# A hybrid decoder step: the decode tokens in the second token group, their state update beside groups three and four

## Chip, cores, metric

The kernel runs on one core of one Trainium2 chip. The metric is the device time of one execution in microseconds (us), as a median over repeated runs.

## What is computed

One inference step of a two-layer decoder on 1040 prompt tokens (16 meta tokens and 1024 own) and 8 decode tokens, one for each of 8 sequences with a state of their own. Layer 0 mixes tokens by a causal convolution, layer 1 by RWKV-7; each is followed by a squared-ReLU MLP (1024 to 4096 to 1024). All data are float32. The part that matters here is the RWKV-7 step, for 16 heads of size 64:

```python
def _wkv7_step(S, inp):
    r_t, w_t, k_t, v_t, kk_t, a_t = inp
    sa = jnp.einsum('bhvk,bhk->bhv', S, -kk_t)
    S = (S * w_t[:, :, None, :] + sa[..., None] * (kk_t * a_t)[:, :, None, :]
         + v_t[..., None] * k_t[:, :, None, :])
    y = jnp.einsum('bhvk,bhk->bhv', S, r_t)
    return S, y
...
r = (xr @ w_r).astype(f32)     # k, v likewise; decay, a and the gate g by low-rank products
...
y = jnp.moveaxis(ys, 0, 1)     # then a norm over each head, a bonus term, the gate and w_o
out = ((yn + bonus).astype(h.dtype) * g) @ w_o
```

For the prompt the state starts at zero and the kernel works in chunks of 64 tokens, with matrix products. For each decode token there is one such step from a given state, `state_wkv` (8 x 16 heads, 64 x 64 each), whose new value is an output.

## The kernel before

**Stages.** Layer 0 (convolution and MLP) takes the first part of the span. Then come the mixers of layer 1 (`mixer_in`, about 1130 to 1840 us), which make r, k, v, decay, rate and gate, and then per token group the output norm, `mixer_out` (w_o) and the second MLP. The features lie on the 128 partitions in 8 blocks (`KT`), the tokens along the free axis.

**Groups.** The mixers take the tokens in four groups (`G1`, L33; the code counts from 0): 272, 256, 256 and 264. The last one holds 256 prompt tokens and the 8 decode tokens. For each group and each feature block p, TensorE multiplies with w_r and w_v, and between these with w_k for the next group (`keys`). Before block 0 come the low-rank products for the gate (`gate`) and, in block 0, those for decay and rate (`decay_rate`); their weights are eight tiles of 256 KB per group (`narrow_w`, L930), loaded from a scratch in DRAM (d_lr) into the pool `wide` with four buffers (L771), gate first. k, the gate and the bonus go to DRAM (d_k, d_g, d_bv); k is fetched again (`fetch`). The operands of the recurrence go to DRAM too (d_ab, d_n, d_v).

**The recurrence.** `chunk(c)` (L1218) is a chain of small products on TensorE with steps on ScalarE and VectorE between them; `front(c)` loads its operands and masks them (ps "A", copies "no" L1198, masks "xa" L1199 and "nr" L1200; "sw" L1266 is the decayed state, a product on GpSimd). `inverses` (L1141) inverts small triangular blocks on VectorE for the four chunks of a group. Chunks, inverses and the output norm (`norm_gate`, L1397) are Python generators. Their pieces are issued between the large products: each fill point in the mixers calls `tick` (L1465), which advances the inverses by one step, the chunks by a credit of 2.0 and the first output norm by one step. A fill point stands before each block's projections and twice in each of them. What is left of the chunks runs beside `mixer_out` and the MLP of the first output group, through `filler`, together with the decode step and the output norms, each stream spread over all its points.

**Order.** On TensorE the instructions keep the order of the program (`manual_schedule`, L1471). On the other engines and DMA queues a planner orders them, by its own estimate of when each is ready; a queue then runs in that order, and an instruction that waits holds up those behind it. Semaphores come from the data dependencies. A tile whose pool has one buffer can be written again only when all readers of the last contents are done.

**Decode.** In the last group the columns behind the prompt (`npr` to `n`) are the decode tokens. Six vectors of each feature block (decay, k, key norm, its product with the rate, r, v) are copied to `ddec` by GpSimd (`dd`, L977). `decode_step` (L1354) then transposes `ddec` (four pieces, PSUM tag "x"), writes them to d_dec in DRAM and loads them again with (sequence, head) on the partitions (dq). Sixteen rounds follow, one for four of the 64 rows of each head's state: load the rows (128 x 256), two products with a sum along the row (`sa`, `yd`), five more products and additions, store. All nine operations are on VectorE (L1383 to L1391), load and store are issued by SyncE. The tiles live in a pool of their own (`dk`) that opens when the step begins.

The functions that the change touches:

Of the kernel before, what the change touches and what calls it, by code (L numbers as in the profile page):

```python
# [16 lines left out]
P = 128  # L17
# [15 lines left out]
G1 = [(0, 272), (272, 256), (528, 256), (784, 264)]  # L33
# [15 lines left out]
def hybrid_step(tc, x_prompt, x_sample, state_conv, state_shift, state_wkv, meta_tokens,  # L49
# [10 lines left out]
    with ctx:  # L60
# [710 lines left out]
        wide = pool(ld, "wided", 4)  # L771
# [6 lines left out]
        open_ep(ld, "d", ey=2)  # L778

# [14 lines left out]
        prep, norm = {}, {}  # L794
        sst = cur["raw"].tile([P, D], F32, name="sst", tag="raw")
# [10 lines left out]
        def shift_out(hx, npr):  # L806

            so = cur["raw"].tile([P, D], F32, name="so", tag="raw")
            for half in range(2):
                pv = bank(f"pso{half}")  # L810
                for q in range(4):
                    nc.tensor.transpose(pv[:DEC + 1, q * P:(q + 1) * P], hx[:, half * 4 + q, npr:npr + DEC + 1], ident)
                nc.scalar.copy(so[:DEC + 1, half * 512:(half + 1) * 512], pv[:DEC + 1, :])
            nc.scalar.dma_start(o_shift_prompt[0], so[0:1, :])
            nc.scalar.dma_start(o_shift_sample[0], so[1:DEC + 1, :])

        def prepare(g):

            c0, n = G1[g]
            npr = min(c0 + n, NP_TOK) - c0  # L820
            nm = lambda s, *a: f"{s}{g}" + "".join(f"_{x}" for x in a)

            hx = hnp.tile([P, KT, 1 + N1], F32, name=nm("hx"), tag="hx")
            if g == 0:
                nc.gpsimd.memset(hx[:, :, 0:1], 0.0)
                nc.sync.dma_start(hx[:, :, 1:1 + n], d_hn[:, :, :n])
            else:
                nc.sync.dma_start(hx[:, :, :1 + n], d_hn[:, :, c0 - 1:c0 + n])
            yield
            xx = hnp.tile([P, KT, N1], F32, name=nm("xx"), tag="xx")  # L830
            for k in range(KT):
                (nc.gpsimd if k % 3 == 2 else nc.vector).tensor_sub(xx[:, k, :npr], hx[:, k, 0:npr], hx[:, k, 1:1 + npr])
                yield
            if npr < n:
                nc.vector.tensor_sub(xx[:, :, npr:n], sps, hx[:, :, 1 + npr:1 + n])
            def mix(i, k):

                t = mixp.tile([P, N1], F32, name=nm("mx", i, k), tag="mx")
                nc.vector.scalar_tensor_tensor(t[:, :n], xx[:, k, :n], vec("x_mix", i * KT + k), hx[:, k, 1:1 + n],
                                               op0=ALU.mult, op1=ALU.add)  # L840
                return t[:, :n]

            prep[g] = mix, hx
# [26 lines left out]
        def keys(g, fill):  # L870

            c0, n = G1[g]
# [24 lines left out]
            split(*r16p, r16[:, :n], nc.vector)  # L897
        carry = {"tail": lambda: None}

        def mixer_in(g, tick):  # L900

            c0, n = G1[g]
            npr = min(c0 + n, NP_TOK) - c0
# [83 lines left out]
            def finish(p, rk, ab, vv):  # L987
                def trace():
# [10 lines left out]
                    pieces = [(i, a0 + i * P, P) for i in range(ncg // 2)] + ([(2, 0, META)] if g == 0 else [])  # L999
                    for i, c1, w in pieces:  # L1000
                        nc.tensor.transpose(pv_[:w, i * P:(i + 1) * P], vv[:, c1:c1 + w], ident)
# [33 lines left out]
                    bv = t_("bv", p, "bv", 2)  # L1035
                    nc.vector.tensor_mul(bv[:, :n], vv[:, :n], pb[:, :n])
                    return lambda: nc.gpsimd.dma_start(d_bv[:, p, c0:c0 + n], bv[:, :n])
# [8 lines left out]
            for p, rk2 in ahead_of(fetch):  # L1046
# [8 lines left out]
                gt = t_("gt", p, "gt", 2)  # L1055
                nc.scalar.copy(gt[:, :n], ps[:, :n])
                nc.scalar.dma_start(d_g[:, p, c0:c0 + n], gt[:, :n])
# [17 lines left out]
                em = t_("em", p, "em", 2)  # L1075
# [54 lines left out]
        st = {"done": -1, "inv": -1, "credit": 0.0, "decoded": False}  # L1130
# [223 lines left out]
        def decode_step():  # L1354

            with ExitStack() as s:
                dk = pool(s, "dk", 1)
                for q in range(4):
                    pt = bank(f"pdd{q}", "x")
                    for i in range(2):  # L1360
                        nc.tensor.transpose(pt[:6 * DEC, i * P:(i + 1) * P],
                                            ddec[:, 2 * q + i].rearrange("p i b -> p (i b)"), ident)
                    dst = tt(f"dst{q}", "t2")[:6 * DEC, :256]
                    nc.scalar.copy(dst, pt[:6 * DEC, :256])
                    nc.scalar.dma_start(d_dec.rearrange("i b d -> (i b) d")[:, q * 256:(q + 1) * 256], dst)
                    yield 3
                dq = dk.tile([P, 6, HS], F32, name="dq")
                nc.scalar.dma_start(dq, d_dec.rearrange("i b (h c) -> (b h) i c", c=HS))
                yield 6
                sa = dk.tile([P, HS], F32, name="sa")  # L1370
                yd = dk.tile([P, HS], F32, name="yd")
                HV = HS // 16
                s_in = state_wkv[0].rearrange("b h v k -> (b h) v k")
                s_out = o_wkv_sample[0].rearrange("b h v k -> (b h) v k")
                rows = lambda t: t.rearrange("p (v k) -> p v k", k=HS)
                for hv in range(HS // HV):
                    vs = slice(hv * HV, (hv + 1) * HV)
                    S = rows(dk.tile([P, HV * HS], F32, name=f"Sdec{hv}", tag="S", bufs=2))
                    t4 = rows(dk.tile([P, HV * HS], F32, name=f"t4{hv}", tag="t4"))
                    nc.sync.dma_start(S, s_in[:, vs, :])  # L1380
                    overv = lambda i: dq[:, i:i + 1, :].broadcast_to([P, HV, HS])
                    overk = lambda t: t.unsqueeze(2).broadcast_to([P, HV, HS])
                    nc.vector.tensor_mul(t4, S, overv(2))  # L1383
                    nc.vector.tensor_reduce(sa[:, vs], t4, axis=AX.X, op=ALU.add)
                    nc.vector.tensor_mul(S, S, overv(0))
                    nc.vector.tensor_mul(t4, overk(sa[:, vs]), overv(3))
                    nc.vector.tensor_add(S, S, t4)
                    nc.vector.tensor_mul(t4, overk(dq[:, 5, vs]), overv(1))
                    nc.vector.tensor_add(S, S, t4)
                    nc.vector.tensor_mul(t4, S, overv(4))  # L1390
                    nc.vector.tensor_reduce(yd[:, vs], t4, axis=AX.X, op=ALU.add)  # L1391
                    nc.sync.dma_start(s_out[:, vs, :], S)
                    yield 4
                nc.scalar.dma_start(d_y[NP_TOK:].rearrange("b (h c) -> (b h) c", c=HS), yd)
                st["decoded"] = True
# [66 lines left out]
        ng0 = norm_gates(GN_OF[0])  # L1462
        PACE = [0, 2.0, 2.0, 2.0]

        def tick(g, slow):  # L1465
# [3 lines left out]
            next(ng0, None)  # L1469

        in_order = lambda: tc.manual_schedule(engines={nc.tensor.engine})  # L1471
        with in_order():
# [7 lines left out]
            carry["tail"]()  # L1480
            while invert():
# [7 lines left out]
        with ExitStack() as l1:  # L1489
# [81 lines left out]
            def group(g, actp, hidp, sums):  # L1571
# [8 lines left out]
                                ([decode_step()], 82), ([norm_gates(GN_OF[1]), ng2], NGA))  # L1580
# [64 lines left out]
```

## Time and profile before

| | us |
|---|---|
| median of 3 runs | 2832.22 (2829.05 to 2835.45) |
| the profiled execution | 2823.53 |
| its span, first to last instruction | 2821.8 |
| mean granted TensorE clock in it | 0.977 of full speed |

The profile is of one execution. PE is TensorE, PEld its weight loads, DVE VectorE, ACT ScalarE, POOL GpSimd, SP SyncE; a q behind a name (SPq, ACTq) marks what the engine's queue issues, such as DMAs. The rows come from these views: the page with 40 equal slices (a digit is the busy share in tenths, PEclk the granted clock in tenths); busy time by stretch (start:end, length, then busy time and number of instructions for each engine, granted clock, share of time that the DMA engines were busy, GB/s); waits (engine, operation, line, what it waited for: us in total, times, the longest); groups (line, engine, operation, output<-inputs, shapes, count | busy us, mean ns of one | idle before, and for what); one line's instructions (count: shortest, median, longest in ns, first and last start); the order in time (start, length, instruction, [idle before <- releaser]); and the chain that ended last, where a DMA's row gives its start and how long it took.

### The profile page before, as it was taken

How to read it: one execution, taken by the hardware profiler on the slowest of the kernel's cores; microseconds unless marked ns; L12 is line 12 of the kernel's file. 1: busy time of each engine (PE TensorE's matmuls, PEld its weight loads, DVE VectorE, ACT ScalarE, POOL GpSimd, SP SyncE). 2: the span in 40 equal slices, each digit the busy share in tenths (PEclk: the TensorE clock that was granted, in tenths of full speed). 3: DMA queues.
4: the chain of work that ended last, by engine and by line, in shares of the span. 5: the costliest groups of instructions: out<-in, count | busy, mean ns of one | idle time of the engine just before them, and what ended most of it. 6: DMA issues, size and time to landing. Idle time of an engine off the chain costs nothing.

```text
span 2821.8 us, 51604 instructions
## 1 busy us (share of the span) xinstructions
PE 2669.5 (95%) x19594; PEld 2521.3 (89%) x19594; DVE 1785.4 (63%) x3586; ACT 1189.5 (42%) x2235; POOL 1520.2 (54%) x2100
## 2 busy tenths in 40 slices
PE   8999999999999899998999999978899999999998
PEld 8999999999999898786877778777899999999998
DVE  5999999996455545234756455588985564444444
ACT  5545444544354343233454454454444452222223
POOL 6686877887788775022212112375568773333332
PEclk9999999999999999999999999989899999999999
DMA  6663544454445642677767766766665542222211
GB/s 179 179 184 87 156 137 134 137 175 137 140 132 162 191 130 82 198 215 201 185 176 211 186 172 178 203 184 167 170 202 155 170 125 87 68 69 73 70 53 42
DMA packets 615862, 416.42 MB, mean 148 GB/s; under 512 B 104936, under 2 KB 558760, under 8 KB 615614
## 3 DMA queue, kind: packets, MB, share of 16 engines
q1 hardware_dynamic: 565996, 367.36, 46.0%
q10 hardware_dynamic: 41090, 19.93, 2.7%
q0 software_dynamic: 8528, 25.83, 2.6%
q8 instruction: 155, 2.54, 0.4%
q14 instruction: 93, 0.76, 0.1%
HBM read 345.60 MB, written 68.37 MB: 147 GB/s over the span
## 4 chain that ended last, share of the span: by engine, by line
PE 71%; DVE 13%; DMA 6%; issue 4%; ACT 3%; POOL 2%; SPq 0%; ACTq 0%; DVEq 0%; POOLq 0%
PE ps_in L187 8%; PE ps_in L189 8%; PE ps_in L188 8%; PE out L187 8%; PE out L189 8%; PE out L188 8%; PE pk L865 3%; PE pr L865 2%; PE pv L865 2%; POOL wo_lo L162 1%; DVE ni L1154 1%; DVE cv L519 1%; PE ps_o L189 1%; DVE tt L1153 1%; PE ps_o L188 1%
## 5 line engine op out<-in xcount | busy, mean ns | idle before, releaser
L162 POOL TENSOR_TENSOR wo_lo<-wo_raw,wo_hi 128x256 fp32r<-128x256 f32 x736 | 566.5, 802 | 267.5 <-ACT wo_hi L157 253.2
L162 POOL TENSOR_TENSOR wi_lo<-wi_raw,wi_hi 128x256 fp32r<-128x256 f32 x640 | 488.9, 796 | 285.8 <-ACT wi_hi L157 265.4
L187 PE MATMUL out<-hh,wo_hi 128*128 128x352 f32 (+2 forms) x1536 | 503.4, 328 | 19.8 <-DVE h L355 9.3
L355 DVE TENSOR_TENSOR h<-h,out 128x352 f32<-128x352 f32 (+2 forms) x768 | 387.7, 511 | 195.9 <-PE out L189 195.2
L189 PE MATMUL out<-hl,wo_hi 128*128 128x352 f32 (+2 forms) x1536 | 494.0, 324 | 7.2 <-DVE hl L141 7.2
L187 PE MATMUL ps_in<-m_h,wi_hi 128*128 128x352 f32 (+2 forms) x1536 | 496.2, 323 | 1.2 <-DVE h L355 1.2
L188 PE MATMUL out<-hh,wo_lo 128*128 128x352 f32 (+2 forms) x1536 | 495.3, 323 | 0.0
L189 PE MATMUL ps_in<-m_l,wi_hi 128*128 128x352 f32 (+2 forms) x1536 | 494.5, 322 | 0.1
L188 PE MATMUL ps_in<-m_h,wi_lo 128*128 128x352 f32 (+2 forms) x1536 | 492.6, 321 | 0.0
L519 DVE SCALAR_TENSOR_TENSOR cv<-u,wdw,cv 128x352 f32<-128x352 f32 (+2 forms) x720 | 377.2, 574 | 0.7
L157 ACT CAST wi_hi<-wi_raw 128x1024 fp32r<-128x1024 f32 x160 | 167.9, 1050 | 388.6 <-PE out L189 198.3
L157 ACT CAST wo_hi<-wo_raw 128x1024 fp32r<-128x1024 f32 x184 | 192.6, 1049 | 318.4 <-PE out L189 153.6
L187 PEld LDWEIGHTS out<-hh,wo_hi 128*128 128x128 f32 x1536 | 293.0, 191 | 26.0 <-DVE h L355 11.6
L189 PEld LDWEIGHTS out<-hl,wo_hi 128*128 128x128 f32 x1536 | 291.2, 190 | 8.9 <-DVE hl L141 8.8
L188 PEld LDWEIGHTS out<-hh,wo_lo 128*128 128x128 f32 x1536 | 292.4, 190 | 0.7
L187 PEld LDWEIGHTS ps_in<-m_h,wi_hi 128*128 128x128 f32 x1536 | 290.1, 189 | 3.2 <-issue 1.7
L188 PEld LDWEIGHTS ps_in<-m_h,wi_lo 128*128 128x128 f32 x1536 | 289.4, 188 | 1.0
L189 PEld LDWEIGHTS ps_in<-m_l,wi_hi 128*128 128x128 f32 x1536 | 288.7, 188 | 1.2 <-DVE m_l L285 0.4
L342 DVE SCALAR_TENSOR_TENSOR r<-ps_in,rs_m 128x352 f32<-128x352 f32 (+2 forms) x192 | 98.4, 516 | 238.7 <-PE ps_in L189 235.0
L141 DVE TENSOR_TENSOR hl<-s,hh 128x352 fp32r<-128x352 f32 (+2 forms) x192 | 147.1, 767 | 106.2 <-ACT hh L140 106.0
L344 ACT ACTIVATE s<-r 128x352 f32<-128x352 f32 (+2 forms) x192 | 93.8, 491 | 129.1 <-DVE r L342 128.5
L865 PE MATMUL pv<-mx,wv_raw 128*128 128x256 f32 (+2 forms) x512 | 125.3, 393 | 2.7 <-ACT rk L1049 2.7
(356 smaller groups left out, 4874.4 us busy)
## 6 DMA issues: line engine op xcount, KB each, us to landing
wi_raw<-in_w_mlp_in_dram SPq DMA_DIRECT2D x160, 512.0 KB
wo_raw<-in_w_mlp_out_dram SPq DMA_DIRECT2D x160, 512.0 KB
wk_raw<-in_rwkv_w_k_dram SPq DMA_DIRECT2D x32, 512.0 KB
wr_raw<-in_rwkv_w_r_dram SPq DMA_DIRECT2D x32, 512.0 KB
wv_raw<-in_rwkv_w_v_dram SPq DMA_DIRECT2D x32, 512.0 KB
d_ab<-ab POOLq DMA_DIRECT2D x32, 512.0 KB, 5.0
pg_raw<-in_conv_w_pw_dram SPq DMA_DIRECT2D x24, 512.0 KB
pa_raw<-in_conv_w_pw_dram SPq DMA_DIRECT2D x24, 512.0 KB
```

Of the source, the lines that this page charges most:

```text
L141: eng_lo.tensor_sub(lo, src, hi.bitcast(F32))
L157: nc.scalar.copy(hi[:, :a * b], raw[:, :a * b])
L162: eng_lo.tensor_sub(lo[:, cs], raw[:, cs], hi[:, cs].bitcast(F32))
L187: nc.tensor.matmul(ps, w[0], act[0], start=first, stop=False)
L188: nc.tensor.matmul(ps, w[1], act[0], start=False, stop=False)
L189: nc.tensor.matmul(ps, w[0], act[1], start=False, stop=last)
L342: nc.vector.scalar_tensor_tensor(r[:, :n], ps[:, :n], 0.0, rs()[:, :n], op0=ALU.max, op1=ALU.mult)
L344: nc.scalar.activation(s[:, :n], r[:, :n], AF.Square)
L355: nc.vector.tensor_add(hv[:, 4 * i + m, :], hv[:, 4 * i + m, :], ps[:, :n])
L519: nc.vector.scalar_tensor_tensor(acc[m][:, :n], ug[:, m, j:j + n], wdw[:, m, j:j + 1], acc[m][:, :n], op0=ALU.mult, op1=ALU.add)
L865: nc.tensor.matmul(ps[:, :n], w[:, k, :], act[k], start=k == 0, stop=k == KT - 1)
L1153: nc.vector.tensor_mul(o, ni[:, :j, j:j + 1].broadcast_to([B, j, wd]), ni[:, j:j + 1, j + 1:top].broadcast_to([B, j, wd]))
```

## The change

The 8 decode tokens leave the last group and join the second (`GD = 1`): the groups are now 272, 256 + 8, 256, 256. Their columns in DRAM are no longer next to the group's own, so each load or store of a whole group becomes two there (`pieces`): hx, d_k written and fetched, d_g, d_bv. `shift_out` runs twice, for the decode tokens in group 1 and for the last prompt token in group 3. `decode_step` becomes a generator that `tick` advances in groups 2 and 3, with a credit of 1.25 per fill point; what is left would run right behind the mixers. Its seven products and additions per round go to GpSimd, the two reductions stay on VectorE. The store of the state is issued by GpSimd. The transposes use the PSUM tag of the projections. The pool `dk` now lives as long as the mixers; `wide` has three buffers instead of four, and bv, gt and em have one instead of two.

```diff
-G1 = [(0, 272), (272, 256), (528, 256), (784, 264)]
+G1 = [(0, 272), (272, 256), (528, 256), (784, 256)]
+GD = 1
...
-        wide = pool(ld, "wided", 4)
+        wide = pool(ld, "wided", 3)
...
         open_ep(ld, "d", ey=2)
+        dk = pool(ld, "dk", 1)
...
+        def extent(g):
+            c0, npr = G1[g]
+            return c0, npr, npr + (DEC if g == GD else 0)
+
+        def pieces(g):
+
+            c0, npr, n = extent(g)
+            return [(slice(0, npr), slice(c0, c0 + npr))] + ([(slice(npr, n), slice(NP_TOK, T))] if n > npr else [])
...
-        def shift_out(hx, npr):
+        def shift_out(hx, lo, n, dst):
...
+            if npr < n:
+                nc.sync.dma_start(hx[:, :, 1 + npr:1 + n], d_hn[:, :, NP_TOK:])
...
-                nc.scalar.dma_start(d_k[:, p, c0:c0 + n], k_[:, :n])
+                for ts, cs in pieces(g):
+                    nc.scalar.dma_start(d_k[:, p, cs], k_[:, ts])
...
-                    bv = t_("bv", p, "bv", 2)
+                    bv = t_("bv", p)
                     nc.vector.tensor_mul(bv[:, :n], vv[:, :n], pb[:, :n])
-                    return lambda: nc.gpsimd.dma_start(d_bv[:, p, c0:c0 + n], bv[:, :n])
+                    return lambda: [nc.gpsimd.dma_start(d_bv[:, p, cs], bv[:, ts]) for ts, cs in pieces(g)]
...
-                nc.sync.dma_start(rk2[:, 1, :n], d_k[:, p, c0:c0 + n])
+                for ts, cs in pieces(g):
+                    nc.sync.dma_start(rk2[:, 1, ts], d_k[:, p, cs])
...
-                gt = t_("gt", p, "gt", 2)
+                gt = t_("gt", p)
                 nc.scalar.copy(gt[:, :n], ps[:, :n])
-                nc.scalar.dma_start(d_g[:, p, c0:c0 + n], gt[:, :n])
+                for ts, cs in pieces(g):
+                    nc.scalar.dma_start(d_g[:, p, cs], gt[:, ts])
...
-                em = t_("em", p, "em", 2)
+                em = t_("em", p)
...
+                if g == GD and p == 0:
+                    shift_out(hx, 1 + npr, DEC, o_shift_sample[0])
                 if g == 3 and p == 2:
-                    shift_out(hx, npr)
+                    shift_out(hx, npr, 1, o_shift_prompt[0])
...
+            eng = nc.gpsimd
+            for hv in range(HS // HV):
+                vs = slice(hv * HV, (hv + 1) * HV)
+                S = rows(dk.tile([P, HV * HS], F32, name=f"Sdec{hv}", tag="S", bufs=2))
+                t4 = rows(dk.tile([P, HV * HS], F32, name=f"t4{hv}", tag="t4"))
+                nc.sync.dma_start(S, s_in[:, vs, :])
+                yield 1
+                eng.tensor_mul(t4, S, overv(2))
+                nc.vector.tensor_reduce(sa[:, vs], t4, axis=AX.X, op=ALU.add)
+                eng.tensor_mul(S, S, overv(0))
+                yield 1
+                eng.tensor_mul(t4, overk(sa[:, vs]), overv(3))
+                eng.tensor_add(S, S, t4)
+                yield 1
+                eng.tensor_mul(t4, overk(dq[:, 5, vs]), overv(1))
+                eng.tensor_add(S, S, t4)
+                nc.gpsimd.dma_start(s_out[:, vs, :], S)
+                yield 1
+                eng.tensor_mul(t4, S, overv(4))
+                nc.vector.tensor_reduce(yd[:, vs], t4, axis=AX.X, op=ALU.add)
+                yield 1
+            nc.scalar.dma_start(d_y[NP_TOK:].rearrange("b (h c) -> (b h) c", c=HS), yd)
...
         def tick(g, slow):
...
+            if g > GD:
+                st["dec"] += 1.25 * slow
+                while st["dec"] > 0 and not st["decoded"]:
+                    st["dec"] -= next(dec, 0)
...
             carry["tail"]()
+            for _ in dec:
+                pass
...
-                                ([decode_step()], 82), ([norm_gates(GN_OF[1]), ng2], NGA))
+                                ([norm_gates(GN_OF[1]), ng2], NGA))
```

The four transposes and the load of dq ahead of the rounds stay as they were, with credits of 3 each and 6.

More of the change, by code (lines that the diff above doesn't have):

```diff
@@ L1354, in decode_step @@
         def decode_step():
[L1356 to L1395, printed above, removed]
@@ new lines, in decode_step @@
+            for q in range(4):
+                pt = bank(f"pdd{q}")
+                for i in range(2):
+                    nc.tensor.transpose(pt[:6 * DEC, i * P:(i + 1) * P],
+                                        ddec[:, 2 * q + i].rearrange("p i b -> p (i b)"), ident)
+                dst = pr.tile([P, N1], F32, name=f"dst{q}", tag="st", bufs=2)[:6 * DEC, :256]
+                nc.scalar.copy(dst, pt[:6 * DEC, :256])
+                nc.scalar.dma_start(d_dec.rearrange("i b d -> (i b) d")[:, q * 256:(q + 1) * 256], dst)
+                yield 3
@@ new lines, in decode_step @@
+            dq = dk.tile([P, 6, HS], F32, name="dq")
+            nc.scalar.dma_start(dq, d_dec.rearrange("i b (h c) -> (b h) i c", c=HS))
+            yield 6
+            sa = dk.tile([P, HS], F32, name="sa")
+            yd = dk.tile([P, HS], F32, name="yd")
+            HV = HS // 16
+            s_in = state_wkv[0].rearrange("b h v k -> (b h) v k")
+            s_out = o_wkv_sample[0].rearrange("b h v k -> (b h) v k")
+            rows = lambda t: t.rearrange("p (v k) -> p v k", k=HS)
+            overv = lambda i: dq[:, i:i + 1, :].broadcast_to([P, HV, HS])
@@ L1397, in norm_gate @@
+            nc.scalar.dma_start(d_y[NP_TOK:].rearrange("b (h c) -> (b h) c", c=HS), yd)
+            st["decoded"] = True
         def norm_gate(units):
@@ L1462, in hybrid_step @@
         ng0 = norm_gates(GN_OF[0])
+        dec = decode_step()
         PACE = [0, 2.0, 2.0, 2.0]
```

30 lines of the change are left out of this document (14 added, 16 removed).

## Prediction

> **What bounds the kernel now.** I read the page first, then the busy time by stretch, then the waits of the stretch that looked worst. The page: TensorE (PE) is busy 95% of the span, so time can only be won where PE stands still or runs at a lowered clock.
>
> ```profile
> span 2821.8 us, 51604 instructions
> PE 2669.5 (95%) x19594; PEld 2521.3 (89%) x19594; DVE 1785.4 (63%) x3586; ACT 1189.5 (42%) x2235; POOL 1520.2 (54%) x2100
> DVE  5999999996455545234756455588985564444444
> PEclk9999999999999999999999999989899999999999
> ```
>
> Slices are 70.5 us. The row of VectorE (DVE) has a plateau of 8 and 9 around 1830 to 2110 us, where PEclk has its only eights. There the decode state update now runs (its first product starts at 1927.6, its last at 2076.7). I set 160 us of it beside 160 us of mixer groups 2 and 3 (the code counts groups from 0), which hold as many chunks of the same recurrence.
>
> ```profile
> core 0: us, PE busy (x) PEld busy (x) DVE busy (x) ACT busy (x) POOL busy (x), PEclk, DMA share, GB/s
> 1425.00:1585.00 160.00, 144.47 (x1502) 120.77 (x1502) 97.84 (x234) 76.33 (x188) 30.30 (x47) 0.98 0.72 194
> 1925.00:2085.00 160.00, 137.31 (x1551) 128.42 (x1550) 148.13 (x315) 71.58 (x148) 83.15 (x94) 0.90 0.62 163
> ```
>
> In the second row DVE is busy 93% (148.13 of 160), PE idles 22.7 us and its clock is 0.90. In the first DVE is at 61%, GpSimd (POOL) at 19%, the clock at 0.98. What PE waits for, in the second stretch and then in the first (us, times, longest):
>
> ```profile
> PE gg L1230 <- ACT no L1198: 8.0, 4, 4.4
> PE Y L1292 <- DVE nr L1200: 5.3, 2, 3.9
> PE yn L1417 <- ACT uv L1278: 4.0, 1, 4.0
> PE gg L1230 <- DVE nr L1200: 2.4, 1, 2.4
> ...
> PE pb L756 <- ACT vv L1067: 5.1, 3, 2.1
> PE yn L1417 <- DVE ey L1446: 2.5, 1, 2.5
> PE gg L1230 <- ACT no L1198: 1.2, 2, 0.7
> ```
>
> These are the recurrence's own steps, each behind a queue on DVE (the ACT copies "no" and "uv" stand between DVE steps). In the mixers the same steps cost PE next to nothing. So the stretch is bound by DVE's queue.
>
> **Part 1: decode leaves DVE in the last layer's MLP.** The nine operations of a round (L1383 to L1391), sixteen rounds, in 1925 to 2085:
>
> ```profile
> L1383 DVE TENSOR_TENSOR t<-Sdec,dq 128x256 f32<-128x256 f32 x16 | 9.5, 596 | 3.1 <-DMA dq<-d_dec 2.9
> L1385 DVE TENSOR_TENSOR Sdec<-Sdec,dq 128x256 f32<-128x256 f32 x16 | 9.5, 592 | 0.0
> L1389 DVE TENSOR_TENSOR Sdec<-Sdec,t 128x256 f32<-128x256 f32 x16 | 9.4, 591 | 0.2
> L1386 DVE TENSOR_TENSOR t<-sa,dq 128x256 f32<-128x256 f32 x16 | 9.4, 587 | 0.1
> L1390 DVE TENSOR_TENSOR t<-Sdec,dq 128x256 f32<-128x256 f32 x16 | 8.8, 548 | 0.2
> L1388 DVE TENSOR_TENSOR t<-dq 128x256 f32<-128x256 f32 x16 | 8.2, 514 | 0.3
> L1387 DVE TENSOR_TENSOR Sdec<-Sdec,t 128x256 f32<-128x256 f32 x16 | 7.9, 496 | 0.1
> L1384 DVE TENSOR_REDUCE sa<-t 128x4 f32<-128x256 f32 x16 | 6.6, 414 | 0.3
> L1391 DVE TENSOR_REDUCE yd<-t 128x4 f32<-128x256 f32 x16 | 6.6, 411 | 0.2
> ```
>
> Seven products and additions make 62.7 us, the reductions 13.2: 75.9 us. Without them DVE has 72 us of work in a stretch that can't be shorter than PE's work, 137.31 x 0.90 = 123.6 us at full clock. So DVE no longer decides; next come the recurrence's chain and PE itself. From the rows: at the mixers' clock PE needs 137.31 x 0.90 / 0.98 = 126.1 us, and I leave it waits of 4.6 us, about what the recurrence and the output norm cost in the mixers (2.5 and 1.2 in the rows, under 1 us in smaller ones). 160 - 126.1 - 4.6 = **29 us gained**. The ends: 36 (160 - 123.6, PE never still), and 20 if PE comes only to the mixers' whole rate (144.47 x 0.98 = 141.6 of 160, so 123.6 x 160 / 141.6 = 139.7). I take 29: most of what holds PE in the mixers, the first wait on "vv", belongs to the mixers alone.
>
> **Part 2: the update in groups 2 and 3.** A round costs five credits, the four transposes 12 and the load of dq 6: 98. Each fill point gives 1.25; group 2 has 8 x 5 + 8 x 2 = 56 (its own projections and the next group's keys), group 3 has 40. So 79 of 96 points do it, the last in the middle of group 3. POOL then has 112 products and additions. Their price there:
>
> ```profile
> L162 POOL TENSOR_TENSOR wo_lo<-wo_raw,wo_hi 128x256 fp32r<-128x256 f32 x42 | 37.8, 927 | 25.1 <-ACT wo_hi L157 16.6 <-issue 5.3 <-DMA out_dram<-Sdec 2.5
> L1383 DVE TENSOR_TENSOR t<-Sdec,dq x16: 406/475/956, 1927.6 to 2076.7; 128x256 f32<-128x256 f32 x16
> L1037 POOL DMA_DIRECT2D d_bv<-bv x32: 555/555/564, 1200.6 to 1836.9; - x32
> ```
>
> 112 x 0.927 = 104 us, plus 16 stores of the state now issued by POOL, 16 x 0.56 = 9 us, beside the 19% it has: over some 300 us it is half busy, so it keeps up. What queues behind a product on POOL (the decayed state "sw", issues of d_ab, d_n, d_bv) waits a microsecond or two; DVE needs "sw" only late in a chunk. DVE keeps the 13 us of reductions and slows: with POOL busy 52% in the MLP (83.15 of 160), products with two SBUF inputs took 0.56 us on average (62.7 / 112) against 0.41 at best, so 70% longer where both run. 104 us x 0.61 = 64 us meet DVE work; if all of it had two SBUF inputs it would lose 64 x 0.41 = 26 us. With the reductions 39 us more on DVE over 300: 61% becomes 74%. What that costs PE I bound by two rows of the mixers:
>
> ```profile
> 1360.00:1380.00 20.00, 20.00 (x178) 17.09 (x177) 19.04 (x47) 10.02 (x27) 4.69 (x8) 1.00 0.87 200
> 1640.00:1660.00 20.00, 16.33 (x126) 12.84 (x124) 11.65 (x28) 14.49 (x35) 2.41 (x5) 0.89 0.53 147
> ```
>
> DVE 95% busy with PE never still, and DVE 58% with PE at 16.33: here DVE's load doesn't set PE's pace. Ends 0 and 39, or 9 at the MLP's rate (36 us of PE time lost for 148 us of DVE). I take **+5**, near the first row.
>
> The Trainium skill ("GPSIMD Engine Reference", Engine selection and Key points) speaks against this part: elementwise work belongs on VectorE, about twice as fast, and the two share SBUF interfaces. By it the work doubles (the 927 against 406 ns above agree), yet it gives no price for an engine that was idle.
>
> **Part 3: one buffer fewer for "wide".** The eight low-rank weight tiles of a group (L930, 256 KB each, four for the gate and four for decay and rate) had four buffers, now three. So the fourth gate tile can start loading only when PE has used the first, and the fourth decay tile likewise. In the fence: PE at the gate, with first, seventh and last k, then a wait in the decay matmuls, SP's issues, and landing times of 256 KB elsewhere.
>
> ```profile
> 1496.27 0.59 PE L943 MATMUL p_g<-hx,g_raw 128*128 128x256 f32 x2
> ...
> 1501.45 0.59 PE L943 MATMUL p_g<-hx,g_raw 128*128 128x256 f32 x2
> ...
> 1502.75 0.60 PE L944 MATMUL p_g<-hx,g_raw 128*128 128x256 f32 x2
> ...
> 1311.37 0.70 PE L943 MATMUL p_wa<-hx,wa_raw 128*128 128x256 f32 x2 [0.41 <-DMA wa_raw<-d_lr]
> 1303.81 2.11 SPq L934 DMA_DIRECT2D wa_raw<-d_lr  x3
> 1994.14 4.24 DMA ey<-d_y
> 2100.71 5.16 DMA ey<-d_y
> ```
>
> From first to seventh k are 5.18 us, so a tile lasts 1.73 and the new load has 3.45 us. It needs an issue (2.11 / 3 = 0.7) and 4.2 to 5.2 us to land; the wait at 1311.37 ends on the second of the three loads, issued about 1304.5: 6.5 us. So PE stands still 0.7 + 4.2 - 3.45 = 1.45 us to 2.45 us, up to 3.75 with the slow one, twice in each of four groups. I take 1.6 x 8 = **+13**, near the low value, since PE waits here and there for ACT and DVE anyway and these catch up meanwhile; ends 0 (all of it made up so) and 30 (3.75 x 8).
>
> **Part 4: the rest.** The extra pieces of group 1 are 16 issues on ACT, 8 on POOL, 9 on SP; ACT's cost most:
>
> ```profile
> L1057 ACTq DMA_DIRECT2D d_g<-gt x32: 326/327/357, 1181.5 to 1822.4; - x32
> 1347.46 0.41 DVE L1036 TENSOR_TENSOR bv<-vv,pk 128x256 f32<-128x256 f32 x1
> 1349.28 0.56 POOL L1037 DMA_DIRECT2D d_bv<-bv  x1 [1.38 <-DVE wa L1092]
> 1367.63 0.41 DVE L1036 TENSOR_TENSOR bv<-vv,pk 128x256 f32<-128x256 f32 x1
> ```
>
> 16 x 0.33 = 5.3 us on ACT, half idle there (76.33 of 160): ends 0 and 5, I take 2. One more shift_out: eight small transposes, an ACT copy pair and a weight buffer held for a moment: 1. Single buffers for bv, gt and em: bv is rewritten 20 us after the last write, and its store was issued 1.8 us after that, so a landing of 5 us is covered; gt and em have the same period. 0; if POOL delayed the issue 13 us, DVE would wait. The eight columns move from 264 + 256 to 256 + 264: 0.
>
> **Sum**: -29 + 5 + 13 + 2 + 1 = **-8 us**. The profiled execution took 2823.53 us (span 2821.8), so 2815.5; the shown runs have a median of 2832.22, 8.7 above it, and there it is 2824.
>
> **Rivals.**
> - **Cheap buffers** (0.2): the loads land before they are needed, or PE makes up the stalls in waits that it has anyway. -29 + 0 + 2 = -27, and up to -36: **2802**.
> - **The gate loads decide** (0.25): with DMA at 72% in the mixers, every late load takes 6.5 us or more: 3.75 x 8 = +30, part 1 yields its low 20, DVE costs 9, the rest 3: +22, **2854**. It turns slower than before when a stall passes (29 - 8) / 8 = 2.6 us. For it: 1311.37. Against: no such wait in the gate itself today.
> - **Shared interfaces** (0.15): POOL's products and DVE's operations hold each other up, and 32 reductions queue on DVE for products behind them: 39 us + 32 x 0.5 = 55 us on DVE, at 0.24 us per us +13 instead of +5: zero, **2832**. The shared interfaces of the Trainium skill ("GPSIMD Engine Reference", Key points) would be the cause.
>
> **Chances.** Forecast 0.4 (2814 to 2834 by itself). About 0.2%, 5.7 us, is what a measurement can tell from no change. Faster: 0.2 + two thirds of the forecast 0.27 = 0.47; same: 0.13 of the forecast and 0.07 of the third rival = 0.20; slower: 0.25 and 0.08 = 0.33. Low end: -36 + 0 = 2796. High: +22 and a few us for the ends of parts 2 and 4: 2858.
>
> **What would show it.** DVE in the MLP behind the mixers near 60% instead of 93%, the waits on "no", "nr", "uv" down to a few us and PEclk at 0.98: part 1 right. PE waiting for g_raw and wa_raw at the seventh k, 1 to 2 us eight times: part 3 right. DVE products with two SBUF inputs longer in groups 2 and 3 without more PE idle: part 2 right. Wrong if PE idles in the MLP without DVE queues, if reductions hold DVE for POOL, or if update rounds are left when the mixers end.

## Result and profile after

The change makes no difference that can be measured: 2833.24 us against 2832.76 us (medians of 12 runs each), ratio 1.0, 95% interval 0.9991 to 1.001. The forecast was -8 us; its range held the time. But 0 is a sum of large terms here, and one of them is not what the prediction said.

The page of the changed kernel (tenths of each of 40 slices; the profiled execution took 2833.61 us):

```profile
span 2831.9 us, 51693 instructions
PE 2673.9 (94%) x19602; PEld 2525.4 (89%) x19602; DVE 1750.3 (62%) x3474; ACT 1194.7 (42%) x2239; POOL 1605.7 (57%) x2236
DVE  5989999996455545233746755668666544444444
PEclk9999999999999999999999999999999999999999
```

The plateau of eights and nines on DVE behind the mixers is gone, and the two eights of PEclk with it. Cut by TensorE's order (a group starts with its first gate product, the next stage with the first w_o product), the execution shows where the time went:

| us | group 0 | 1 | 2 | 3 | w_o to end of recurrence | to second w_o | rest |
|---|---|---|---|---|---|---|---|
| before | 135.2 | 199.4 | 202.9 | 141.3 | 240.5 | 152.1 | 588.6 |
| after | 137.8 | 212.4 | 226.2 | 143.5 | 212.3 | 152.0 | 581.2 |

The mixers are 41 us longer, most of it in group 2 (+23) and group 1 (+13); what follows is 36 us shorter. (The remaining 5 us between these two executions lie ahead of the mixers, where little was changed: the first gate starts at 1166.4 instead of 1161.7.)

Busy time by stretch, after: groups 1 and 2, and the stage from w_o to the end of the recurrence. Then the same three of before:

```profile
core 0: us, PE busy (x) PEld busy (x) DVE busy (x) ACT busy (x) POOL busy (x), PEclk, DMA share, GB/s
1304.20:1516.60 212.40, 189.30 (x1851) 157.72 (x1850) 114.55 (x294) 91.01 (x239) 51.35 (x113) 0.95 0.70 177
1516.60:1742.80 226.20, 191.40 (x2029) 159.36 (x2028) 149.74 (x304) 99.11 (x244) 131.63 (x188) 0.94 0.69 188
1886.30:2098.60 212.30, 196.91 (x2256) 183.95 (x2256) 157.93 (x306) 113.00 (x226) 135.97 (x170) 0.96 0.64 166
```
```profile
1296.90:1496.30 199.40, 180.26 (x1811) 151.36 (x1810) 114.11 (x294) 89.19 (x229) 34.38 (x58) 0.97 0.74 188
1496.30:1699.20 202.90, 185.91 (x2022) 155.23 (x2021) 116.80 (x273) 95.05 (x239) 39.29 (x60) 0.97 0.71 189
1840.50:2081.00 240.50, 208.06 (x2264) 194.26 (x2265) 218.29 (x445) 114.97 (x230) 145.22 (x170) 0.91 0.63 166
```

Behind the mixers TensorE did the same work in 28 us less: 196.91 x 0.96 = 189 us at full clock in 212.3 us, against 208.06 x 0.91 = 189 in 240.5. (The stretch from 1925 to 2085 us that the prediction looked at holds other work now, since the mixers end 46 us later.) In group 2 it is the other way round: idle time went from 202.9 - 185.9 = 17.0 us to 226.2 - 191.4 = 34.8, at a clock of 0.94 instead of 0.97, while DVE got 33 us more and POOL 92. All sixteen rounds had run before group 3 began at 1742.8: the planner, which orders every engine but TensorE by readiness, moved them forward. Their first product, first sum and last product, in the view of single lines (count: shortest, median, longest in ns, first and last start), with the waits before or behind them (us, times):

```profile
L1398 POOL TENSOR_TENSOR t<-Sdec,dq x16: 716/726/3294, 1563.9 to 1719.1; 128x256 f32<-128x256 f32 x16
  DVE yd L1410: 10.2, 8
```
```profile
L1399 DVE TENSOR_REDUCE sa<-t x16: 390/414/421, 1566.7 to 1721.3; 128x4 f32<-128x256 f32 x16
  POOL t L1398: 7.5, 6
...
  POOL t L1402: 6.7, 4
```
```profile
L1409 POOL TENSOR_TENSOR t<-Sdec,dq x16: 734/736/1230, 1574.9 to 1730.4; 128x256 f32<-128x256 f32 x16
  DVE yd L1410: 8.7, 4
```

POOL waited 10.2 us for the second sums of the rounds before, whose tile t it writes again, and 6.7 us for the first sum of its own round. DVE stood 7.5 us for POOL ahead of the first sums and 8.7 ahead of the second ones. All four are new: before, one engine did it all. What TensorE waited for in group 2 (us in total, times, longest), after and then before:

```profile
PE pn L891 <- ACT sq L900: 6.9, 2, 6.0
PE gg L1245 <- ACT no L1213: 6.1, 4, 2.7
PE yn L1435 <- DVE ey L1464: 6.0, 1, 6.0
PE pb L757 <- DVE n L1031: 3.5, 1, 3.5
PE S L1300 <- DVE uv L1292: 3.4, 2, 2.8
```
```profile
PE pn L880 <- ACT sq L888: 3.0, 1, 3.0
PE yn L1417 <- DVE ey L1446: 2.5, 1, 2.5
...
PE gg L1230 <- ACT no L1198: 1.3, 2, 0.7
PE S L1285 <- DVE uv L1277: 0.6, 1, 0.6
```

"no" and "uv" are steps of the recurrence that held TensorE in the MLP of before too. The output norm (ey) and the mixers' own steps are late as well. Which of these came with the rounds is seen below, in the kernel without them.

### The profile page after: what moved, and what is told of

It is laid out like the page before. It is cut to its first block, busy times and chain, and to the rows that moved or that the text cites. A ratio compares the mean times of both kernels' runs of the same rounds, so it can differ in the third digit from the quotient of the medians.

```text
span 2831.9 us, 51693 instructions
## 1 busy us (share of the span) xinstructions
PE 2673.9 (94%) x19602; PEld 2525.4 (89%) x19602; DVE 1750.3 (62%) x3474; ACT 1194.7 (42%) x2239; POOL 1605.7 (57%) x2236
## 4 chain that ended last, share of the span: by engine, by line
PE 73%; DVE 11%; DMA 5%; POOL 4%; issue 4%; ACT 3%; ACTq 0%; SPq 0%; DVEq 0%; POOLq 0%
PE out L188 8%; PE out L190 8%; PE ps_in L188 8%; PE ps_in L190 8%; PE out L189 8%; PE ps_in L189 8%; PE pk L876 3%; PE pv L876 3%; PE pr L876 3%; DVE cv L520 2%; PE A L1207 1%; POOL wi_lo L163 1%; DVE mx L850 1%; PE ps_oo L188 1%; DMA hx<-d_hn 1%
## 5 line engine op out<-in xcount | busy, mean ns | idle before, releaser
L876 PE MATMUL pk<-mx,wk_raw 128*128 128x256 f32 (+2 forms) x512 | 129.1, 401 | 1.1 <-ACT vv L1080 1.1
```

The lines of the kernel that those rows point to most:

```text
L876: nc.tensor.matmul(ps[:, :n], w[:, k, :], act[k], start=k == 0, stop=k == KT - 1)
```

## Experiments

Times are medians, ratios those to the kernel before in the same batch, with the 95% interval; 0.1% is 2.8 us. Theory at the start: the gain behind the mixers is real and is spent again in the mixers, on the loads of the low-rank weights and on the rounds. Rival: the gain is missing because DVE wasn't the limit there.

### The loads and the moved columns, each alone

```diff
-        wide = pool(ld, "wided", 4)
+        wide = pool(ld, "wided", 3)
```

> The kernel before with three buffers for the low-rank weights instead of four, and nothing else. My theory (the loads are a good half of what the mixers lose): 10 to 18 us slower than before, with TensorE waiting for g_raw and wa_raw in most groups. Rival one (the rounds of the state update lose the time): 0 to 5 us. Rival two (the moved columns and split transfers lose it): 0 to 5 us.

Measured: 2839.39 us, 1.0024 (1.0011 to 1.0037), +7 us. The waits of TensorE in its mixers:

```profile
PE p_g L943 <- DMA g_raw<-d_lr: 7.4, 2, 6.4
PE p_wa L943 <- DMA wa_raw<-d_lr: 5.6, 3, 3.1
```

So a load is late in five places, in two of them by 6.4 and 3.1 us and else by little, not in eight by 1.6. The waits come to 13.0 us, as much as was forecast, but the kernel lost only 7 (3 to 10). Whether TensorE made up the rest in waits that it has anyway, or the profiled execution (2845.9 us, the slowest of ten) had more of them than most, isn't shown.

The second kernel is that of before with the decode columns in group 1: the constants, `extent`, `pieces` and `shift_out` of the change, and nothing else of it.

> The kernel before with the decode columns in group 1, the split transfers and the two calls of shift_out; four buffers for the low-rank weights, two for bv, gt and em, and the state update on VectorE in the last MLP as before. My theory: within 5 us of before. Rival one (rounds): the same. Rival two (columns and split transfers): 15 us slower or more.

Measured: 2837.74 us, 1.0018 (1.0007 to 1.003), +5 us (2 to 8), where the prediction had 2 + 1.

### The rounds left out, after and before

```diff
-            for hv in range(HS // HV):
+            for hv in range(0):
...
+            nc.vector.tensor_copy(yd, dq[:, 0])
```

> The changed kernel without the sixteen rounds of the state update: their loads, products, sums and stores are left out, so the decode tokens' new state and output are not computed. What the rounds cost in the mixers is the difference to the changed kernel. My theory (rounds cost 5 to 10 us): 5 to 10 us faster than the changed kernel, group 2 still some 10 us longer than before. Rival one (rounds cost most of the mixers' loss of 41 us): 25 to 30 us faster than the changed kernel, group 2 as long as before. Rival two: as my theory, with group 1 still 13 us longer.

Measured: 2811.24 us, 0.9924 (0.9899 to 0.9949). So in the changed kernel the rounds cost 0.76%, 22 us (14 to 29): more than the 5 to 10 expected, less than the rival's 25 to 30. Group 2 takes 209.3 us instead of 226.2; group 1 is still 208.6. TensorE's waits in group 2, behind the longest one (for "vv"):

```profile
PE yn L1436 <- DVE ey L1465: 5.1, 1, 5.1
PE pn L891 <- ACT sq L900: 3.0, 1, 3.0
PE S L1300 <- DVE uv L1292: 2.7, 1, 2.7
PE gg L1245 <- ACT no L1213: 0.6, 2, 0.4
```

The waits for "ey" and "uv" are there without the rounds as well. What the rounds brought along is the wait for "no" (6.1 us against 0.6) and part of that for "sq" (6.9 against 3.0).

The kernel before without its rounds, by the same edit:

> The kernel before without the sixteen rounds of the state update in the last MLP: loads, products, sums and stores are left out, so the decode tokens' new state and output are not computed. It measures what taking the rounds off VectorE there is worth by itself. My forecast for that part was 29 us; the runs so far leave 34 or so. Theory (the recurrence waits behind VectorE's queue): 25 to 36 us faster than before, the waits on no, nr and uv nearly gone. Rival (the time lies in TensorE's own work or in the loads): under 15 us faster.

Measured: 2799.5 us, 0.9887 (0.9868 to 0.9906): where they stood before, the rounds cost 32 us (27 to 37). That is all that part 1 could gain, and it refutes the rival. With 29 predicted, part 1 holds.

The terms add up: -32 (rounds out of the MLP) + 7 (buffers) + 5 (columns) + 22 (rounds in the mixers) = +2 us, measured 0. Nothing is left for the single buffers of bv, gt and em, as predicted, but the intervals of the terms leave room for some 10 us.

### Why do the rounds cost 22 us in the mixers?

The products on DVE again:

```diff
-            eng = nc.gpsimd
+            eng = nc.vector
```

> The changed kernel with the seven products and additions of a round on VectorE instead of GpSimd. If GpSimd and VectorE holding each other up costs group 2 its time: 5 us faster than the changed kernel or more, since a product takes 0.4 to 0.5 us on VectorE against 0.73 on GpSimd and the reductions no longer wait. If VectorE's queue in the mixers has little room: 5 to 20 us slower. My theory: within 5 us of the changed kernel.

Measured: 2829.16 us, 0.999 (0.998 to 1.0): within 5 us of the changed kernel, as expected. Group 2 takes 225.3 us against 226.2 with GpSimd. Group 2 with the rounds left out, then with the products on DVE:

```profile
1510.00:1719.30 209.30, 188.24 (x2029) 158.11 (x2028) 117.75 (x273) 98.93 (x245) 37.08 (x60) 0.95 0.70 187
```
```profile
1514.40:1739.60 225.20, 190.97 (x2029) 158.70 (x2028) 171.27 (x416) 97.46 (x243) 46.10 (x76) 0.95 0.71 191
```

With the products on DVE, DVE has 53.5 us more than without rounds; with the products on GpSimd (149.74) it still has 32.0. The sums are 13.1 of these. The other 19 are DVE's own operations that got longer. One of them in group 2, with the rounds left out, on DVE, on GpSimd (behind the bar: busy us, mean ns):

```profile
L1117 DVE TENSOR_TENSOR ab<-rk,ex 128x512 f32<-128x512 f32 x8 | 5.5, 683 | 0.0
```
```profile
L1117 DVE TENSOR_TENSOR ab<-rk,ex 128x512 f32<-128x512 f32 x8 | 5.4, 681 | 0.0
```
```profile
L1117 DVE TENSOR_TENSOR ab<-rk,ex 128x512 f32<-128x512 f32 x8 | 8.5, 1058 | 0.0
```

The same instruction takes 681 ns beside DVE's own products and 1058 beside GpSimd's. By the Trainium skill ("GPSIMD Engine Reference", Key points) the engines share SBUF interfaces and contend when a DVE instruction has two SBUF inputs; these rows agree.

The two sums of each round left out (sa and yd filled once):

```diff
-                nc.vector.tensor_reduce(sa[:, vs], t4, axis=AX.X, op=ALU.add)
...
-                nc.vector.tensor_reduce(yd[:, vs], t4, axis=AX.X, op=ALU.add)
```

> The changed kernel without the two sums of a round on VectorE (both tiles are filled once from dq), so GpSimd's products and VectorE no longer wait for each other; the decode tokens' state and output are wrong by it. If the hand-over between the two engines costs group 2 its time: 10 to 20 us faster than the changed kernel. If shared interfaces to SBUF do: VectorE's operations in group 2 stay as slow, and the time is within 7 us of the changed kernel.

Measured: 2824.92 us, 0.9973 (0.9963 to 0.9982): -8 us, between the bounds of the two theories. The sums, with the handing back and forth between DVE and POOL, are a third of the price. Group 2, and the same instruction as above in it:

```profile
1513.10:1733.50 220.40, 190.10 (x2029) 159.01 (x2028) 140.44 (x274) 99.68 (x245) 132.69 (x188) 0.93 0.72 196
L1117 DVE TENSOR_TENSOR ab<-rk,ex 128x512 f32<-128x512 f32 x8 | 7.0, 874 | 0.0
```

TensorE's wait for "no" is down to 0.6 us, as without the rounds. But VectorE, with no sums to do, is still busy 23 us more than without the rounds (140.44 against 117.75), and the group 11 us longer (220.4 against 209.3). So of the 17 us that the rounds add to group 2, some 6 go with the sums and the hand-over and 11 stay with GpSimd's products and the transfers, by one execution each.

All rounds on one state tile, with 15 loads and 16 stores left out:

```diff
+            S = rows(dk.tile([P, HV * HS], F32, name="Sdec", tag="S", bufs=2))
+            nc.sync.dma_start(S, s_in[:, 0:HV, :])
...
-                nc.sync.dma_start(S, s_in[:, vs, :])
...
-                nc.gpsimd.dma_start(s_out[:, vs, :], S)
```

> The changed kernel with all sixteen rounds on one tile of state rows that is loaded once: 15 loads and 16 stores of the state (4 MB) are left out, so the new state is not written and the decode output is wrong. The rounds cost 21 us in the mixers, of which the sums and their hand-over were 8. If the rest lies in DMA traffic beside the mixers' own: 7 to 13 us faster than the changed kernel. If in products on GpSimd slowing VectorE: within 4 us of the changed kernel.

Measured: 2829.64 us, 0.9978 (0.9962 to 0.9995): about -6 us, between the bounds of the two theories, and group 2 is as long as ever (226.0). Inconclusive: the transfers may cost some us. The edit also ties the rounds closer together, since all of them now use one tile: POOL waits 16.4 us for the second sums, instead of 10.2.

Four buffers for "wide" again, paid for with one state tile, t in the pool of the k tiles and sa per round:

```diff
-        wide = pool(ld, "wided", 3)
+        wide = pool(ld, "wided", 4)
...
-                S = rows(dk.tile([P, HV * HS], F32, name=f"Sdec{hv}", tag="S", bufs=2))
-                t4 = rows(dk.tile([P, HV * HS], F32, name=f"t4{hv}", tag="t4"))
+                S = rows(dk.tile([P, HV * HS], F32, name=f"Sdec{hv}", tag="S"))
+                t4 = rows(pr.tile([P, N1], F32, name=f"t4{hv}", tag="st", bufs=2)[:, :HV * HS])
...
```

> The changed kernel with four buffers for the low-rank weights again. To make room the state's rows have one buffer instead of two, the products' tile comes from the pool of k, and the first sum is kept for one round only; so rounds can't overlap and spread over more of groups 2 and 3. Theory: groups 0 and 1 come back by 6 to 8 us (the loads); if a round costs time because the rounds are packed into group 2, spreading gives another 5 to 15 us; together 8 to 20 us faster than the changed kernel. Rival (the price of a round is the same wherever chunks run): only the 6 to 8 us of the loads.

Measured: 2836.31 us, 1.0009 (0.9996 to 1.0022), so not faster than the changed kernel, against both theories. Group 1 came back from 212.4 to 207.6 us, but the rounds now wait for their loads, the last one starts at 1784.4, and group 3 went from 143.5 to 154.1 us. By these stages the rounds took what the loads gave.

That left open whether the rounds are dear because the planner bunched them in group 2. So each round was tied to TensorE's order by a small product:

```diff
+                pg = bank(f"pgate{hv}")
+                nc.tensor.matmul(pg[:, :HS], ident, dq[:, 2, :], start=True, stop=True)
+                kg = dk.tile([P, 1, HS], F32, name=f"kg{hv}", tag="kg")
+                nc.scalar.copy(kg.rearrange("p i x -> p (i x)"), pg[:, :HS])
-                eng.tensor_mul(t4, S, overv(2))
+                eng.tensor_mul(t4, S, kg.broadcast_to([P, HV, HS]))
```

> The changed kernel, but each of the sixteen rounds is held back by a small product on TensorE, which keeps the order of the program: it copies the key row of dq through PSUM (128x64) and ScalarE into the tile that the round's first product reads. So the rounds can't be pulled forward by the planner; they stand one by one from about a third of group 2 to the end of group 3, as the prediction had them. Theory packing (the rounds cost 22 us instead of the predicted 5 because they run bunched in group 2, ahead of the recurrence's steps): spread, they cost 5 to 10 and the time is 2816 to 2822 us, ratio 0.994 to 0.996, with group 2 down from 226 to about 215 us and group 3 up by at most 5. Theory load (a round costs its 1.4 us wherever it runs in the mixers): 2830 to 2838 us, ratio 0.998 to 1.002, and what group 2 gains group 3 loses. The gates themselves: sixteen products of 64 columns and sixteen small copies, at most 3 us.

Measured: 2828.53 us, 0.9989 (0.9979 to 0.9998). The first product's row, and groups 2 and 3 by stretch:

```profile
L1402 POOL TENSOR_TENSOR t<-Sdec,kg x16: 724/741/1057, 1577.0 to 1804.9; 128x256 f32<-128x256 f32 x16
```
```profile
1511.99:1728.85 216.86, 190.52 (x2051) 159.41 (x2050) 137.00 (x293) 100.01 (x256) 99.25 (x144) 0.96 0.72 190
1728.85:1882.44 153.59, 130.92 (x1279) 108.96 (x1277) 91.44 (x203) 66.75 (x178) 57.33 (x87) 0.93 0.69 187
```

The rounds stood where the prediction had them, up to the middle of group 3. Group 2 gave 9.3 us back and group 3 took 10.1. So the bunching isn't the main cause: spreading is worth 3 us, at most 6, and a round still costs over a microsecond. What the gates themselves cost wasn't measured; the longest wait of TensorE that the trace puts down to them took 3.7 us.

### Another place for the rounds

Before, with the decode step behind the last chunk of the recurrence, in the same stream:

```diff
-                                ([until(NCH - 1)], FA * CHUNK_WAIT * (NCH - 1 - st["done"])),
-                                ([decode_step()], 82), ([norm_gates(GN_OF[1]), ng2], NGA))
+                                ([until(NCH - 1), decode_step()], FA * CHUNK_WAIT * (NCH - 1 - st["done"]) + 30), ([norm_gates(GN_OF[1]), ng2], NGA))
```

> The kernel before with the decode step in the stream of the recurrence, behind its last chunk, instead of beside it; engines and buffers as before. Theory (rounds cost time only where chunks of the recurrence stand in the same VectorE queue): 15 to 33 us faster than before, with the last products running behind the last chunk and the next w_o stage not later for them. Rival (75 us of VectorE work costs about the same wherever it is put): within 6 us of before. A third way: the rounds end too late for the last output norm, and what the stage wins is lost at the next: within 10 us of before, with a gap ahead of the second w_o stage.

Measured: 2832.96 us, 1.0003 (0.9993 to 1.0013). The recurrence ends after 199.0 us instead of 240.5, and the next stage takes 205.3 instead of 152.1. One wait, and the stretch around it:

```profile
PE yn L1417 <- DVE ey L1446: 27.0, 1, 27.0
```
```profile
2163.00:2203.00 40.00, 13.50 (x83) 13.49 (x84) 29.70 (x64) 9.36 (x19) 8.74 (x12) 0.66 0.35 101
```

The output norm of the last tokens needs the rounds' result, and its transposes stand in TensorE's fixed order: 41 us are gained, and 53 paid in the next stage, 27 of them in this one wait. (The rest of the span is 7 us shorter, 581.2 instead of 588.6.)

So the last output norm was let go at the fourth fill point of the second w_o stage, which has two for each feature block (`last`, `dec` and `ng1` are the generators that stood in the filler):

```diff
-                st["decoded"] = True
...
+            last, dec, ng1 = until(NCH - 1), decode_step(), norm_gates(GN_OF[1])
             fill, rest = filler(2 * KT + MLP_POINTS,
-                                ([until(NCH - 1)], FA * CHUNK_WAIT * (NCH - 1 - st["done"])),
-                                ([decode_step()], 82), ([norm_gates(GN_OF[1]), ng2], NGA))
+                                ([last, dec], FA * CHUNK_WAIT * (NCH - 1 - st["done"]) + 30), ([ng1, ng2], NGA))
...
-                for _ in rest:
+                for _ in chain(last, dec, ng1):
...
-            mixer_out(1, residp2, actp, fill, add)
+            calls = []
+
+            def fill1():
+                calls.append(0)
+                st["decoded"] = len(calls) > 3
+                fill()
+            with in_order():
+                mixer_out(1, residp2, actp, fill1, add)
```

> As b_late (the kernel before with the decode step behind the last chunk), but the output norm of the last tokens, which needs the decode result, moves behind the third feature block of the second w_o stage, and TensorE keeps program order there. b_late lost 27 us in one wait of TensorE for that norm. Theory (the rounds cost little where no chunk runs; the gap ate the gain): 15 to 30 us faster than before. Rival (75 us of VectorE work cost the same everywhere, the gap was that price): the wait shows again at another place, within 6 us of before.

Measured: 2816.19 us, 0.9938 (0.9915 to 0.9961), 18 us faster than before. TensorE no longer stops there, though DVE is full up to 2163. Then two of the seven products and additions of a round became ScalarE copies with a scale per row (t5 is a tile of its own):

```diff
-                    nc.vector.tensor_mul(t4, overk(sa[:, vs]), overv(3))
+                    for j in range(HV):
+                        nc.scalar.activation(t4[:, j, :], dq[:, 3, :], AF.Copy, scale=sa[:, hv * HV + j:hv * HV + j + 1])
...
-                    nc.vector.tensor_mul(t4, overk(dq[:, 5, vs]), overv(1))
+                    for j in range(HV):
+                        nc.scalar.activation(t5[:, j, :], dq[:, 1, :], AF.Copy, scale=dq[:, 5, hv * HV + j:hv * HV + j + 1])
+                    nc.vector.tensor_add(S, S, t5)
```

> As b_tail, with two of the seven products of a round (sum times vector, value times key) on ScalarE, as four scaled copies of 64 elements each, so VectorE has 16 x 2 x 0.42 = 13 us less there. Theory: 3 to 10 us faster than b_tail, since VectorE was the full engine behind the last chunk in b_late. Rival (VectorE isn't the limit there, or the longer hand-over eats it): within 3 us of b_tail.

Measured: 2807.45 us, 0.991 (0.9891 to 0.9929), 25 us faster than before, and the fastest of the kernels that compute everything. The kernel before without rounds had 0.9887, so the rounds cost some 7 us here (0.23%). Two stretches of the former, then of this one:

```profile
2123.00:2163.00 40.00, 34.45 (x221) 32.75 (x220) 39.49 (x81) 13.99 (x19) 31.26 (x39) 1.00 0.55 161
2163.00:2203.00 40.00, 36.80 (x235) 35.08 (x235) 35.95 (x74) 13.02 (x17) 32.07 (x39) 1.00 0.52 157
```
```profile
2123.00:2163.00 40.00, 38.10 (x249) 37.33 (x248) 36.11 (x75) 26.46 (x71) 33.09 (x41) 1.00 0.59 183
2163.00:2203.00 40.00, 37.82 (x246) 36.67 (x244) 28.60 (x58) 21.62 (x44) 35.34 (x45) 1.00 0.57 170
```

DVE falls from 39.49 to 36.11 and from 35.95 to 28.60 of 40, ScalarE, busy 14 and 13 of 40 us, takes it, and TensorE rises from 34.45 to 38.10 and from 36.80 to 37.82.

## Why the prediction was right, and where it was not

The time lay in the range, but the range was wide, 2796 to 2858 us, and that the sum came so near is partly luck: the errors of the terms have both signs. Of the three outcomes the prediction gave "same" the smallest chance, 0.20.

- **What bounds** was read rightly: DVE's queue behind the mixers. Without the rounds the kernel is 32 us faster.
- **Part 1** (29 us, ends 20 and 36): 32 measured, some 7 of them not in the stretch of the rounds but from the second w_o stage on (588.6 against 581.2 in the table; 581.3 in the kernel of before without rounds). The prediction didn't look there. From w_o to the end of the recurrence the clock rose from 0.91 to 0.96, and the waits on "no" and "nr" fell as foretold, before and after:

```profile
PE gg L1230 <- ACT no L1198: 9.5, 6, 4.4
PE Y L1292 <- DVE nr L1200: 9.0, 3, 3.9
```
```profile
PE Y L1307 <- DVE nr L1215: 5.6, 3, 3.6
...
PE gg L1245 <- ACT no L1213: 1.3, 3, 0.7
```

  DVE came to 74% in this stage (157.93 of 212.3), not near 60%.
- **Part 2** (+5, ends 0 and 39) is the step that failed: 22 us (14 to 29). What was mis-sized is the price of DVE's load in the mixers. "Here DVE's load doesn't set PE's pace" rested on two windows of 20 us, and so 39 us more on DVE were put at 5. The load itself was foretold about rightly: DVE got 32 us more in group 2. But the group became 17 us longer by it, about half a microsecond for each. With the products on DVE, the rounds cost 0.9990 - 0.9924 = 0.66%, 19 us (11 to 26). Their nine operations add up to 62.6 us there (75.9 in the MLP), so the rate is 0.30 us per us (0.18 to 0.42). That is about the one of 0.24 that the prediction had from the MLP and laid aside as the dearer one. (All that a round brings is in these rates, its loads and stores too.) The prediction had named the signs: part 2 right if PE doesn't idle more in groups 2 and 3, wrong if reductions hold DVE for POOL. PE idled 34.8 us in group 2 instead of 17.0, and DVE stood 16 us for POOL. GpSimd was counted as relief. It took load off DVE (32.0 us more instead of 53.5), but group 2 is as long with it as without. The sums and their hand-over account for 8 of the 22 us, the transfers perhaps for 6; how the rest divides between longer DVE operations and GpSimd's queue stays open. The place of the rounds, in group 2 and not up to the middle of group 3, was foretold wrongly too, but the spread kernel shows that it hardly matters.
- **Part 3** (+13): 7 (3 to 10). The mechanism was right, loads that come late; the size was off. TensorE's waits for these loads in the changed kernel, in order of time:

```profile
1317.60 0.81 PE L954 MATMUL p_g<-hx,g_raw 128*128 128x264 f32 x1 [6.74 <-DMA g_raw<-d_lr]
1333.89 0.49 PE L954 MATMUL p_wa<-hx,wa_raw 128*128 128x264 f32 x1 [0.71 <-DMA wa_raw<-d_lr]
1536.26 0.48 PE L954 MATMUL p_wa<-hx,wa_raw 128*128 128x256 f32 x1 [0.43 <-DMA wa_raw<-d_lr]
1765.56 0.79 PE L954 MATMUL p_wa<-hx,wa_raw 128*128 128x256 f32 x1 [3.35 <-DMA wa_raw<-d_lr]
```

  They sum to 11.2 us, in four places of the eight, and two of these make up 10 of it. So the sum of the waits was near the forecast in both kernels with three buffers, but not their form, and not all of it reached the time.
- **Part 4** (+3): 5 (2 to 8) for the columns and the second shift_out, nothing measurable for the single buffers.
- **Rivals.** Cheap buffers and gate loads fell: +7 lies between 0 and +30. (The sum of the first left out the +5 of part 2; with it, it is -29 + 5 + 0 + 3 = -21.) The third, shared interfaces, gave the time that came (2832) and a mechanism that is there (681 against 1058 ns, and engines that wait for each other); but it priced the rounds at 13 us where they cost 22, and its sum came out only because part 3 was smaller and part 1 larger.

Against the forecast of -8 the measured terms differ by -3 (part 1), +17 (part 2), -6 (part 3) and +2 (part 4), which gives the +2 of the experiments. Each of the measured terms is known to some us only.

## What to carry to other kernels

Work that holds up a chain takes much of its price along when it moves to another stretch in which the same chain runs (here 22 of 32 us); the price is to be counted at the rate measured where it stands, unless a stretch as long as the work, not a short window, shows another. An idle engine is no free one when its partner must wait for it and its operations stretch the partner's. The rounds grew cheap, some 7 us instead of 32, only where the recurrence had ended, with their one reader moved out of TensorE's way and part of them on an engine with room.

## What the runs showed of the hardware

- GpSimd products of 128 x 256 took 0.61 to 0.74 us in the median of their line beside DVE work, against 0.93 us for the split of the weights (L162) from which the price was taken (on DVE the same products took 0.42 to 0.48 us in the mean); a DVE product with two SBUF inputs took 55% longer beside them (1058 against 681 ns).
- Around TensorE's 27 us gap the granted clock averaged 0.66 over 40 us. The Trainium skill ("TensorE: Matmul & The Clock Gate", Part 1) says that an idle window of about 3.4 us halves the clock: an estimate by it, with the clock halved for as long as the gap lasts, is 1 - 0.5 x 27 / 40 = 0.66, and the trace agrees.
- Executions of the same part differ: the first gate of the mixers started between 1161.7 and 1164.9 us in the kernel before and its four variants that differ from it only behind the mixers. One profiled execution each can't settle a difference of 3 us.
